# Sixteen adaLN modulation modules computed as row dot products on VectorE, from weights laid out by output column

## The chip, the cores and the metric

The kernel runs on one core of a Trainium2 chip. A core has a matrix engine (TensorE, PE in the profile), VectorE (DVE), ScalarE (ACT), GpSimd (POOL) and SyncE (SP), which here only issues transfers. The metric is the time of one execution on the device, in microseconds; the kernel before took 1797.8 us in the median of three runs.

## The reference, cut to what matters

Two layers of a diffusion backbone work on 256 latent tokens and 256 context tokens of 1024 features. Each layer is a half-step SwiGLU, a token mixing of four head groups, and another half-step SwiGLU. Each of these is modulated by nine vectors of 1024 (a shift, a scale and a gate for each of three sub-layers), one set from the condition `c` for the latent tokens and one from `c_ctx` for the context:

```python
for l in range(DEPTH):
    mx = jnp.split((jax.nn.silu(c) @ w_mod[l] + b_mod[l])[:, None, :], N_MOD, axis=-1)
    mz = jnp.split(jax.nn.silu(c_ctx) @ w_mod[l] + b_mod[l], N_MOD, axis=-1)
    x = x + 0.5 * mx[2] * swiglu(modulate(rms_norm(x), mx[0], mx[1]), ffn1_w1[l], ffn1_w3[l], ffn1_w2[l])
    z = z + 0.5 * mz[2] * swiglu(modulate(rms_norm(z), mz[0], mz[1]), ffn1_w1[l], ffn1_w3[l], ffn1_w2[l])
    ...   # token mixing with mx[3..5], second SwiGLU with mx[6..8]
```

`w_mod[l]` is a matrix of 1024 x 9216. So a modulation module (one of nine vectors of one layer) is a product of two rows of 1024 with a matrix of 1024 x 1024, 4 MB of f32 weights for very little arithmetic.

## The kernel before, in words

The activations lie transposed: features on the 128 partitions (eight tiles, `X[0]` to `X[7]`), 512 tokens along the free dimension. All large products are done in three passes: each weight tile and each activation is split into a high part (`whi`, `hh`, `gh`) and a low part (`wlo`, `hl`, `gl`), and `product` (L278 to L285) adds high x high, low x high and high x low in PSUM.

Weights come as one stream (`w_load` at L237 on SP's queue, three raw buffers); `w_conv` casts the high part on ACT (L248) and subtracts it on DVE for the low part (L251), some tiles ahead of the product that takes them.

In the SwiGLU (`ffn`) the 22 hidden tiles go in two groups of 12 and 10. For each hidden tile PE does the gate and the up projection (48 products), and `finish` applies silu on ACT (L408), multiplies on DVE (L410) and splits the result. Then for each of the eight output tiles PE does the down projection (36 products in the first group, 30 in the second) and DVE adds the result to `X` (L480).

Two of the eighteen modules, the shift and the scale of the very first norm, are computed at the start by PE (`mods_load`, `mods_first`). The other sixteen are the subject here. They are a generator, `mod_modules`, that runs in the background of three SwiGLUs: `step` takes two steps of it after each hidden tile and two after each down-projection tile. The first SwiGLU of layer 0 computes six modules, its second one four, the first SwiGLU of layer 1 six.

A module (`mod_module`) takes nine steps. In each of the first eight it loads 128 rows of the weights (a tile `wmod` of 128 x 1024, L163, three buffers) and adds them, scaled by the silu of the condition's feature on that partition, to an accumulator `macc` of 128 x 1024, for `c` and for `c_ctx`: the first time by a scaled copy on ACT (L166), then by multiply-adds on DVE (L169). What is left is a sum over partitions. The ninth step does it on PE: four products with ones (L174), a copy on ACT (L177), four transposes that bring the output column onto the partition (L180), and the bias on DVE (L184).

The order of instructions on each engine is made by a scheduler with a cost model of its own, from the program order, priorities and a few pins; `issue_after(behind())` puts the module's DVE instructions behind the latest low part of a weight.

Of the kernel before, what the change touches and what calls it, by code (L numbers as in the profile page):

```python
# [7 lines left out]
F32 = mybir.dt.float32  # L8
F32R = mybir.dt.float32r
U8 = mybir.dt.uint8  # L10
AF = mybir.ActivationFunctionType
ALU = mybir.AluOpType
# [3 lines left out]
P = 128  # L16
D = 1024
KD = 8
S = 256
T = 512  # L20
# [41 lines left out]
def bmid(ap, n):  # L62
    a = [list(x) for x in ap.ap]
    return bass.AP(tensor=ap.tensor, offset=ap.offset, ap=a[:-1] + [[0, n]] + a[-1:])
# [3 lines left out]
def tile_backbone(ctx: ExitStack, tc: tile.TileContext, a: dict, out: bass.AP):  # L68
    nc = tc.nc
# [7 lines left out]
    def bank(tag, name):  # L77
        return mm.tile([P, 512], F32, tag=tag, name=name, bufs=BANKS[tag])
# [4 lines left out]
    def small(n, name):  # L83
        return sp.tile([P, n], F32, tag=name, name=name, bufs=2 if name[0] in "de" else 8)

# [1 line left out]
    cin = cp.tile([P, KD, 32], F32, name="cin")  # L87
    nc.scalar.dma_start(out=cin, in_=a["cin"])
    cst = cp.tile([P, C_N], F32, name="cst")
# [1 line left out]
    bmod = cp.tile([P, 2, 72], F32, name="bmod")  # L91
# [21 lines left out]
    ident = cst[:, C_ID:C_ID + 128]  # L113
    ones = cp.tile([P, 128], F32, name="ones")
# [4 lines left out]
    sc = cin  # L119
# [1 line left out]

    mods = [cp.tile([P, 72, 2], F32, name=f"mod{l}") for l in range(2)]

# [1 line left out]
    def mods_load(q, pool, tiles):  # L125
        for k in range(KD):
            tag, n = ("wmod", 3) if q == 3 and k % 2 else (("gh", FA) if (q * KD + k) % 2 else ("gl", FA))
            if q < 3:
                raw = pool.tile([P, T], F32R, tag=tag, name="wfirst", bufs=FA).bitcast(F32)
            else:  # L130
                if k % 2 == 0:
                    raw2 = pool.tile([P, 2, 512], F32, tag="macc" if k == 0 else "wmod", name="wfirst", bufs=2 if k == 0 else 3)
                raw = raw2[:, k % 2, :]
            v = a["w_mod"][0, k * P:(k + 1) * P, 256 * q:256 * q + 256]
            nc.sync.dma_start(out=raw.rearrange("p (m c) -> p m c", m=2),
                              in_=bass.AP(tensor=v.tensor, offset=v.offset, ap=[list(v.ap[0]), [D, 2], list(v.ap[1])]))
            tiles.append(raw)
            yield
# [17 lines left out]
                                    in0=pt[:, :P].rearrange("p (m i s) -> p m i s", m=2, i=2)[:, :, :, 0:2],  # L156
                                    in1=bc(bmod[:, 0, 0:16].rearrange("p (m a i) -> p a m i", m=2, a=4)[:, q], 2), op=ALU.add)

    def mod_module(l, m, pool, behind):
        acc = pool.tile([P, 2, D], F32, tag="macc", name="macc", bufs=2)  # L160
        for k in range(KD):
            raw = pool.tile([P, 2, 512], F32, tag="wmod", name="wmod", bufs=3).rearrange("p a b -> p (a b)")
            nc.sync.dma_start(out=raw, in_=a["w_mod"][l, k * P:(k + 1) * P, m * D:(m + 1) * D])  # L163
            for s in range(2):
                if k == 0:
                    nc.scalar.activation(acc[:, s], raw, AF.Copy, scale=sc[:, k, s:s + 1])  # L166
                else:
                    with tc.issue_after(behind()):
                        nc.vector.scalar_tensor_tensor(out=acc[:, s], in0=raw, scalar=sc[:, k, s:s + 1], in1=acc[:, s],  # L169
                                                       op0=ALU.mult, op1=ALU.add)  # L170
            yield
        pm = bank("B", "pm")
        for j in range(4):
            nc.tensor.matmul(pm[32 * j:32 * j + 32, :], ones[:, 0:32], acc[:, j // 2, (j % 2) * 512:(j % 2) * 512 + 512],  # L174
                             start=True, stop=True)
        sb = pool.tile([P, T], F32, tag="g", name="modsb", bufs=2)
        nc.scalar.copy(sb, pm)  # L177
        pt = bank("B", "pmt")
        for i in range(4):
            nc.tensor.transpose(pt[:, i * P:(i + 1) * P], sb[:, i * P:(i + 1) * P], ident)  # L180
        dst = mods[l][:, 8 * m:8 * m + 8, :]
        src = pt.rearrange("p (i s j x) -> p s j i x", i=4, s=2, j=2)
        for s in range(2):
            nc.vector.tensor_tensor(out=dst.rearrange("p (j i) s -> p s j i", j=2)[:, s], in0=src[:, s, :, :, 0],  # L184
                                    in1=bmod[:, l, 8 * m:8 * m + 8].rearrange("p (j i) -> p j i", j=2), op=ALU.add)
        if m in (2, 8):
            nc.vector.tensor_scalar(out=dst, in0=dst, scalar1=0.5, scalar2=None, op0=ALU.mult)
        yield
# [1 line left out]
    def mcol(l, m, d, s):  # L190
        return mods[l][:, 8 * m + d, s:s + 1]

# [1 line left out]
    wlist = []  # L194

    def ffn_units(l, f):
# [10 lines left out]
    for l in range(2):  # L207
        ffn_units(l, 1)
        for u in ORDER:
# [6 lines left out]
            elif u in "RNQF":  # L216
                name, n = {"F": ("wfou", 2), "R": ("wgr", 2), "N": ("wna", 6), "Q": ("wgqa", 4)}[u]
# [8 lines left out]
    wlo = [None]  # L226
# [36 lines left out]
            w_load()  # L263
        return ready.pop(0)

# [1 line left out]
    def split_tiles(d):  # L267
        return (xp.tile([P, T], F32R, tag=f"hh{d}", name=f"hh{d}"),
                xp.tile([P, T], F32R, tag=f"hl{d}", name=f"hl{d}"))
# [23 lines left out]
        wh, wl = w[:2]  # L293
        product(((wh[:, k, :], xh), (wh[:, k, :], xl), (wl[:, k, :], xh)), ps, first, last)

# [1 line left out]
    def norm_square(st, pool, d, s0, s1, eng=nc.gpsimd):  # L297
        c = slice(s0 * S, s1 * S)
        if d == 0:
# [87 lines left out]
        st["apply"] = apply  # L387
        return st

# [1 line left out]
    def down_order(ns, split):  # L391
        tail = split if ns > 1 else 0
        return ([(mt, 0, ns) for mt in range(KD - tail)] +
# [86 lines left out]
            nc.vector.scalar_tensor_tensor(out=X[mt][:, c], in0=py[:, c], scalar=mcol(l, m, mt, s),  # L480
                                           in1=X[mt][:, c], op0=ALU.mult, op1=ALU.add)

# [1 line left out]
    def mixing(l, st, pool, npool):  # L484
        last = l == 1
        ntx = 2 if last else 4
# [56 lines left out]
            nc.vector.tensor_tensor(out=ov, in0=ps, in1=bc(rs[:, :n].rearrange("p (t h) -> p t h", t=2), 64), op=ALU.mult)  # L543
            return o

# [1 line left out]
        g = {}  # L547

        def gates():
# [168 lines left out]
                nc.vector.tensor_tensor(out=gr, in0=gr, in1=nn.rearrange("p (t n) -> p t n", t=2), op=ALU.mult)  # L718
                yield

# [1 line left out]
        def rev(ap):  # L722
            return ap.rearrange("p (b c) -> p b c", c=64)[:, :, ::-1]

# [122 lines left out]
            nc.scalar.copy(hh[:, c], src[:, c])  # L847
            eng.tensor_tensor(out=hl[:, c], in0=src[:, c], in1=hh[:, c].bitcast(F32), op=ALU.subtract)

# [1 line left out]
        nqT = [big(f"nqT{i}", tag=f"T{i}", bufs=1) for i in range(2)]  # L851
        nkS = [pool.tile([P, T], F32R, name=f"nkS{i}", bufs=1) for i in range(4)]
        nv = {}
# [44 lines left out]
                                           lambda e, t: head_bias(2 * hp + e, t), nqT[hp])  # L898
                    deliver(2 + hp, nqT[hp], p, nc.gpsimd)

# [1 line left out]
        def gq_norm(ps, nh, roff, rope):  # L902
            nn = rms_tok(ps, nh)
            w = nh * 64
# [45 lines left out]
                    yield from attend_pair(TAGS[1], p, [(gqT[kv], 0), (gqT[kv], 1)], [gkS[kv]] * 2, [vs] * 2, None, o)  # L950
                    deliver(6 + kv, o, p, nc.vector)

# [1 line left out]
        def fourier_in(U):  # L954
            U["c"] = [big("fou") for _ in range(2)]
            nc.sync.dma_start(out=U["c"][0], in_=a["fou"][:, F_L:F_L + 512])
# [38 lines left out]
            nc.scalar.copy(hh[:, :nx], pt[:, :nx])  # L995
            nc.vector.tensor_tensor(out=hl[:, :nx], in0=pt[:, :nx], in1=hh[:, :nx].bitcast(F32), op=ALU.subtract)

# [1 line left out]
        active = []  # L999

        def background():
# [44 lines left out]
        for i, u in enumerate(ORDER):  # L1046
# [5 lines left out]
            if u in streams:  # L1052
                gen, r = streams[u]
# [24 lines left out]
            evac(l, 5, mt, py, s0, s1)  # L1078
            after(mt, s0, s1)

# [1 line left out]
    def mod_modules(ms, pool):  # L1082
        for l, m in ms:
            yield from mod_module(l, m, pool, lambda: wlo[0])

    npool = ctx.enter_context(tc.tile_pool(name="norm", bufs=1))
    st = {"merge": False}
# [47 lines left out]
                ffn(l, 6, st2, n2, fp, npool, mod_modules([(0, 8)] + [(1, m) for m in range(3)], fp), fin)  # L1135


# [1 line left out]
def _constants():  # L1139
    import numpy as np  # L1140

# [38 lines left out]
def _arrays(inp):  # L1180
    import numpy as np

    g = {k: np.asarray(v) for k, v in inp.items()}
    f32 = np.float32
    r = {}
    xt = np.concatenate([g["x"][0], g["ctx"][0]], axis=0).T
    r["xin"] = xt.reshape(KD, P, T).transpose(1, 0, 2)
    cin = np.zeros((P, KD, 32), f32)
    cin[:, :, 0] = g["c"][0].reshape(KD, P).T
    cin[:, :, 1] = g["c_ctx"].reshape(KD, P).T  # L1190
    r["cin"] = cin
    r["w_mod"] = g["w_mod"]
    r["bmod"] = g["b_mod"].reshape(2, 72, P).transpose(2, 0, 1)

    def feat(w, c0, n, m):
        w = w[:, :, c0:c0 + n]
        return w.reshape(2, KD, P, n // m, m).transpose(0, 3, 2, 1, 4).reshape(2, n // m, P, KD * m)

    def tok(w, c0):
        w = w[:, :, c0:c0 + 256]  # L1200
        return w.reshape(2, 2, 4, P, 256).transpose(0, 1, 3, 2, 4).reshape(2, 2, P, 1024)

    for f in (1, 2):
        for w in (1, 3):
            r[f"f{f}w{w}"] = feat(g[f"ffn{f}_w{w}"], 0, NF * P, P)
        w2 = g[f"ffn{f}_w2"]
        r[f"f{f}w2"] = w2.reshape(2, NF, P, KD, P).transpose(0, 3, 2, 1, 4)
    w = g["w_in"]
    r["wgate"] = feat(w, 1792, 32, 32)[:, 0]
    r["wgqk"] = feat(w, 1024, 256, P)  # L1210
    r["wgv"], r["wgr"] = tok(w, 1280), tok(w, 1536)
    r["wna"] = np.concatenate([tok(w, c) for c in (256, 512, 768)], axis=1)
    r["wgqa"] = np.concatenate([tok(w, c) for c in (1824, 2080)], axis=1)
    r["wfou"] = tok(w, 0)
    r["wout"] = feat(g["w_out"], 0, D, P)
    vec = np.zeros((P, 2, 4), f32)
    row = np.zeros((2, P, R_N), f32)
    wg = np.zeros((P, 2, 2, 128), f32)
    for l in range(2):
        vec[:, l, V_NAQ] = np.tile(g["na_q_norm"][l], 2)  # L1220
        vec[:, l, V_NAK] = np.tile(g["na_k_norm"][l], 2)
        vec[:, l, V_BF] = g["gla_b_gate_f"][l]
        vec[:, l, V_BB] = g["gla_b_gate_b"][l]
        row[l, :, R_GQ:R_GQ + 256] = np.tile(g["gqa_q_norm"][l], 4)
        row[l, :, R_GK:R_GK + 128] = np.tile(g["gqa_k_norm"][l], 2)
        row[l, :, R_GN:R_GN + 256] = np.tile(g["gla_norm"][l], 4)
        for j in range(0, P, 32):
            wg[j:j + 16, l, 0] = g["gla_w_gate_f"][l]
            wg[j + 16:j + 32, l, 1] = g["gla_w_gate_b"][l]
    r["vec"], r["row"], r["wg"] = vec, row, wg  # L1230
    r["na_rpb"] = g["na_rpb"]
    r["cst"], r["fou"], r["lvl"] = _constants()
    return {k: np.ascontiguousarray(v) for k, v in r.items()}
# [19 lines left out]
```

## Time and profile before

| | |
|---|---|
| three runs | 1796.78, 1797.80, 1801.82 us (median 1797.8) |
| span of the profiled execution | 1797.1 us; the page gives no other time of it |
| PE busy | 1738.8 us (97%) |
| DVE busy | 1075.0 us (60%) |
| ACT busy | 703.8 us (39%) |
| mean granted TensorE clock | 0.989 of 2.4 GHz |
| chain that ended last | PE 90%, DMA 4%, DVE 3%, ACT 1% |
| transfers | 250.91 MB, 140 GB/s over the span |

The span runs from the first to the last instruction of one execution that the hardware profiler recorded. An engine's busy time counts the time in which one of its instructions was under way; PE's instructions overlap, so their mean durations don't add up to busy time, and the distance from one start to the next is the better measure of what one costs.

### The profile page before, as it was taken

What the parts mean: (1) busy time and instruction counts of PE and PEld (TensorE: products, weight loads), DVE (VectorE), ACT (ScalarE), POOL (GpSimd) and SP (SyncE); (2) the same over time, 40 slices, a digit from 0 to 9 for tenths busy, and PEclk for the clock granted to TensorE, in tenths of its full rate; (3) what the DMA queues carried; (4) which work ended last, traced back from release to release, by engine and by line L of the source; (5) the groups of instructions that cost most, each with busy time, mean ns of one, the idle gap of its engine ahead of it and who ended that gap; (6) DMA issues with size and microseconds to landing.
All of it is one profiled execution on the core that took longest, in us unless ns stands there. A gap on an engine that the chain in (4) does not pass through costs nothing.

```text
span 1797.1 us, 28107 instructions
## 1 busy us (share of the span) xinstructions
PE 1738.8 (97%) x11334; PEld 1484.1 (83%) x11334; DVE 1075.0 (60%) x1560; ACT 703.8 (39%) x1167; POOL 216.4 (12%) x259
## 2 busy tenths in 40 slices
PE   7999999998989999999999999999999897999999
PEld 5887888786978788887888888887888796889999
DVE  3566766635776667667333477676743476655554
ACT  4432233235645454322222343323223464554443
POOL 1000000012563230000000210000001344220000
PEclk9999999999999999999999999999999999999999
DMA  9455665334221136655332356566523333136664
GB/s 341 155 180 164 206 199 176 105 90 112 77 67 34 41 124 199 188 152 165 104 96 67 105 194 197 162 189 205 180 76 87 91 105 92 49 107 196 178 193 138
DMA packets 91843, 250.91 MB, mean 140 GB/s; under 512 B 17600, under 2 KB 28096, under 8 KB 91712
## 3 DMA queue, kind: packets, MB, share of 16 engines
q1 hardware_dynamic: 90128, 247.79, 45.6%
q8 instruction: 89, 1.46, 0.3%
q10 hardware_dynamic: 1584, 1.32, 0.2%
q14 instruction: 42, 0.34, 0.1%
HBM read 248.02 MB, written 1.05 MB: 139 GB/s over the span
## 4 chain that ended last, share of the span: by engine, by line
PE 90%; DMA 4%; DVE 3%; ACT 1%; issue 1%; POOL 1%; SPq 0%; POOLq 0%; DVEq 0%; ACTq 0%
PE p L285 47%; PE py L285 23%; PE pt L285 7%; PE pyo L285 3%; DMA bias<-in_na_rpb_dram 2%; PE pf L285 1%; PE po L790 1%; PE pm L174 1%; PE prT L781 1%; DVE wlo L251 1%; PE sc L758 1%; DMA wfirst<-in_w_mod_dram 1%; PE pg L554 1%; PE pa L674 1%; ACT whi L248 0%
## 5 line engine op out<-in xcount | busy, mean ns | idle before, releaser
L248 ACT CAST whi<-raw 128x1024 fp32r<-128x1024 f32 (+3 forms) x358 | 339.6, 950 | 826.3 <-PE p L285 297.3
L251 DVE TENSOR_TENSOR wlo<-raw,whi 128x1024 fp32r<-128x1024 f32 (+3 forms) x358 | 396.4, 1109 | 261.3 <-ACT whi L248 255.8
L285 PE MATMUL p<-hl,whi 128*128 128x512 f32 (+1 forms) x1504 | 528.5, 353 | 2.1 <-DVE hl L368 1.4
L285 PE MATMUL p<-hh,wlo 128*128 128x512 f32 (+1 forms) x1504 | 528.3, 352 | 0.0
L285 PE MATMUL p<-hh,whi 128*128 128x512 f32 (+1 forms) x1504 | 525.6, 353 | 1.3 <-ACT hh L363 1.1
L285 PEld LDWEIGHTS p<-hh,whi 128*128 128x128 f32 x1504 | 283.7, 190 | 47.0 <-issue 5.6
L285 PEld LDWEIGHTS p<-hl,whi 128*128 128x128 f32 x1504 | 285.9, 190 | 40.9 <-DVE hl L368 1.8
L285 PEld LDWEIGHTS p<-hh,wlo 128*128 128x128 f32 x1504 | 286.0, 190 | 37.5 <-DVE mod L155 0.2
L169 DVE SCALAR_TENSOR_TENSOR macc<-wmod,cin,macc 128x1024 f32<-128x1024 f32 x224 | 276.6, 1279 | 0.0
L285 PE MATMUL py<-gh,whi 128*128 128x512 f32 (+1 forms) x764 | 266.5, 350 | 0.0
L285 PE MATMUL py<-gl,whi 128*128 128x512 f32 (+1 forms) x764 | 265.5, 348 | 0.0
L285 PE MATMUL py<-gh,wlo 128*128 128x512 f32 (+1 forms) x764 | 265.2, 348 | 0.0
L312 POOL TENSOR_TENSOR ss<-ss,sq 128x512 f32<-128x512 f32 (+1 forms) x34 | 40.7, 1196 | 1095.6 <-ACT sq L309 1094.2
L410 DVE TENSOR_TENSOR g<-p,sl 128x512 f32<-128x512 f32 (+1 forms) x88 | 54.9, 624 | 187.3 <-PE p L285 174.6
L285 PEld LDWEIGHTS py<-gh,whi 128*128 128x128 f32 x764 | 143.4, 188 | 24.6 <-ACT whi L248 3.4
L285 PEld LDWEIGHTS py<-gl,whi 128*128 128x128 f32 x764 | 143.3, 188 | 20.4 <-issue 1.7
L285 PEld LDWEIGHTS py<-gh,wlo 128*128 128x128 f32 x764 | 143.5, 188 | 20.2 <-issue 0.8
L285 PE MATMUL pt<-whi,hl 128*128 128x256 f32 x448 | 132.3, 295 | 9.9 <-POOL hl L366 9.9
L285 PE MATMUL pt<-whi,hh 128*128 128x256 f32 x448 | 132.1, 295 | 0.5 <-DVE nm L762 0.5
L285 PE MATMUL pt<-wlo,hh 128*128 128x256 f32 x448 | 131.8, 294 | 0.0
L480 DVE SCALAR_TENSOR_TENSOR X<-py,mod,X 128x256 f32<-128x256 f32 x112 | 50.3, 480 | 105.0 <-PE py L285 104.8
L285 PEld LDWEIGHTS pt<-whi,hl 128*128 128x128 f32 x448 | 88.4, 197 | 19.5 <-POOL hl L366 13.6
(221 smaller groups left out, 1763.3 us busy)
## 6 DMA issues: line engine op xcount, KB each, us to landing
wmod<-in_w_mod_dram SPq DMA_DIRECT2D x128, 512.0 KB, 3.7
raw<-in_f1w_dram SPq DMA_DIRECT2D x88, 512.0 KB, 4.3
raw<-in_f2w_dram SPq DMA_DIRECT2D x88, 512.0 KB, 3.7
raw<-in_f1w_dram SPq DMA_DIRECT2D x32, 384.0 KB, 3.6
raw<-in_f2w_dram SPq DMA_DIRECT2D x32, 384.0 KB, 3.2
raw<-in_f1w_dram SPq DMA_DIRECT2D x32, 320.0 KB, 2.9
raw<-in_f2w_dram SPq DMA_DIRECT2D x32, 320.0 KB, 3.0
wfirst<-in_w_mod_dram SPq DMA_DIRECT2D x32, 256.0 KB, 6.5
```

What stands on the lines that cost most here:

```text
L169: nc.vector.scalar_tensor_tensor(out=acc[:, s], in0=raw, scalar=sc[:, k, s:s + 1], in1=acc[:, s], op0=ALU.mult, op1=ALU.add)
L174: nc.tensor.matmul(pm[32 * j:32 * j + 32, :], ones[:, 0:32], acc[:, j // 2, (j % 2) * 512:(j % 2) * 512 + 512], start=True, stop=True)
L248: nc.scalar.copy(hi[:, :k * n], raw[:, :k * n])
L251: wlo[0] = nc.vector.tensor_tensor(out=lo[:, :k * n], in0=raw[:, :k * n], in1=hi[:, :k * n].bitcast(F32), op=ALU.subtract).ins
L285: nc.tensor.matmul(ps, w, x, start=first and i == 0, stop=last and i == len(parts) - 1)
L312: (nc.vector if d == KD - 1 else eng).tensor_tensor(out=st["ss"][:, c], in0=st["ss"][:, c], in1=sq[:, c], op=ALU.add)
L410: nc.vector.tensor_tensor(out=g[:, :n], in0=p3[:, :n], in1=sl[:, :n], op=ALU.mult)
L480: nc.vector.scalar_tensor_tensor(out=X[mt][:, c], in0=py[:, c], scalar=mcol(l, m, mt, s), in1=X[mt][:, c], op0=ALU.mult, op1=ALU.add)
L554: nc.tensor.matmul(pg[j:j + 32, :], wf[:, k, :], h[k][0].bitcast(F32), start=k < 4, stop=4 < k)
L674: nc.tensor.matmul(pa[w * b:w * b + w, c * w:c * w + w], ke[hs, k0:k0 + w], qe[hs, q0:q0 + w], start=True, stop=True)
L758: nc.tensor.matmul(ps[:, :n], q[:, e, (t % 2) * P:(t % 2 + 1) * P], ks[e][:, T - n:T], start=i == 0, stop=i == 1)
L781: nc.tensor.transpose(pt[:, c * P:(c + 1) * P], pr[e][:, (2 * half + i) * P:(2 * half + i + 1) * P], ident)
```

## The change: what it does

The weights of the sixteen modules are laid out anew on the host, transposed: for a module and a tile of 128 output columns, the output column is on the partition and the 1024 input features lie along the row (`wmodt`). The condition is brought in as a row of 1024 for `c` and one for `c_ctx`, copied to all 128 partitions by one transfer (`crow`, 1 MB in SBUF), and its silu is taken on ACT, once in each of the three SwiGLUs. A module's step then loads one tile of 128 x 1024 and, for each of the two conditions, multiplies it by the row and sums along the row with one DVE instruction (`tensor_tensor_reduce`, which stands on DVE as two: the product and sum, and the read of the accumulator). Its result is a single column of 128 outputs, which is already where the modulation is used. The ninth step only adds the bias. The ones products, the copy, the transposes and the scaled copies on ACT are gone. The two modules at the start read their part of the weights from an array of their own (`wmodf`).

```diff
-    def mod_module(l, m, pool, behind):
-        acc = pool.tile([P, 2, D], F32, tag="macc", name="macc", bufs=2)
-        for k in range(KD):
-            raw = pool.tile([P, 2, 512], F32, tag="wmod", name="wmod", bufs=3).rearrange("p a b -> p (a b)")
-            nc.sync.dma_start(out=raw, in_=a["w_mod"][l, k * P:(k + 1) * P, m * D:(m + 1) * D])
+    def mod_module(l, m, pool, crow, behind):
+        acc = pool.tile([P, 2, KD], F32, tag="macc", name="macc", bufs=2)
+        for i in range(KD):
+            raw = pool.tile([P, D], F32, tag="wmod", name="wmod", bufs=3)
+            nc.sync.dma_start(out=raw, in_=a["wmodt"][l, m, i])
             for s in range(2):
-                if k == 0:
-                    nc.scalar.activation(acc[:, s], raw, AF.Copy, scale=sc[:, k, s:s + 1])
-                else:
-                    with tc.issue_after(behind()):
-                        nc.vector.scalar_tensor_tensor(out=acc[:, s], in0=raw, scalar=sc[:, k, s:s + 1], in1=acc[:, s],
-                                                       op0=ALU.mult, op1=ALU.add)
+                prod = pool.tile([P, D], F32, tag="mprod", name="mprod", bufs=2)
+                with tc.issue_after(behind()):
+                    nc.vector.tensor_tensor_reduce(out=prod, in0=raw, in1=crow[:, s], scale=1.0, scalar=0.0,
+                                                   op0=ALU.mult, op1=ALU.add, accum_out=acc[:, s, i:i + 1])
             yield
-        pm = bank("B", "pm")
-        for j in range(4):
-            nc.tensor.matmul(pm[32 * j:32 * j + 32, :], ones[:, 0:32], acc[:, j // 2, (j % 2) * 512:(j % 2) * 512 + 512],
-                             start=True, stop=True)
-        sb = pool.tile([P, T], F32, tag="g", name="modsb", bufs=2)
-        nc.scalar.copy(sb, pm)
-        pt = bank("B", "pmt")
-        for i in range(4):
-            nc.tensor.transpose(pt[:, i * P:(i + 1) * P], sb[:, i * P:(i + 1) * P], ident)
         dst = mods[l][:, 8 * m:8 * m + 8, :]
-        src = pt.rearrange("p (i s j x) -> p s j i x", i=4, s=2, j=2)
-        for s in range(2):
-            nc.vector.tensor_tensor(out=dst.rearrange("p (j i) s -> p s j i", j=2)[:, s], in0=src[:, s, :, :, 0],
-                                    in1=bmod[:, l, 8 * m:8 * m + 8].rearrange("p (j i) -> p j i", j=2), op=ALU.add)
+        nc.vector.tensor_tensor(out=dst.rearrange("p i s -> p s i"), in0=acc, in1=bmid(bmod[:, l, 8 * m:8 * m + 8], 2), op=ALU.add)
...
     def mod_modules(ms, pool):
+        crow = pool.tile([P, 2, D], F32, name="crow", bufs=1)
+        v = a["crow"]
+        nc.sync.dma_start(out=crow, in_=bass.AP(tensor=v.tensor, offset=v.offset, ap=[[0, P], [D, 2], [1, D]]))
+        nc.scalar.activation(crow, crow, AF.Silu)
         for l, m in ms:
-            yield from mod_module(l, m, pool, lambda: wlo[0])
+            yield from mod_module(l, m, pool, crow, lambda: wlo[0])
...
-    r["w_mod"] = g["w_mod"]
+    r["crow"] = np.stack([g["c"][0], g["c_ctx"]])
+    r["wmodf"] = g["w_mod"][0, :, :2 * D]
+    r["wmodt"] = g["w_mod"].reshape(2, D, 9, KD, P).transpose(0, 2, 3, 4, 1)
```

The scheduler orders the new program anew. Three places show what moved. On PE in the first SwiGLU, before, where the first module ends (`p` is a gate or up projection's PSUM tile, `hh` and `hl` the split activations):

```order
L285 MATMUL p_1177<-hl_632,whi 128x512
L285 MATMUL p_1177<-hh_631,wlo 128x512
L174 MATMUL pm<-macc,ones 32x512 x4
L285 MATMUL p_1266<-hh_289,whi 128x512
...
L285 MATMUL p_1266<-hl_632,whi 128x512
L180 MATMUL pmt<-cst,modsb 128x128 x4
L285 MATMUL p_1266<-hh_631,wlo 128x512
```

In the changed kernel the rows of L174 and L180 are gone, sixteen of each kind of group, and the products between them follow each other.

On DVE in the first down projection of layer 0, before (`X` is the residual update, `wlo` a weight's low part):

```order
L480 SCALAR_TENSOR_TENSOR X_83<-py,mod_97,X_83 128x256 x2
L251 TENSOR_TENSOR wlo<-raw,whi 128x768
L169 SCALAR_TENSOR_TENSOR macc<-wmod,cin,macc 128x1024 x4
L251 TENSOR_TENSOR wlo<-raw,whi 128x768
L480 SCALAR_TENSOR_TENSOR X_84<-py,mod_97,X_84 128x256 x2
```

And now, at the same place:

```order
L466 SCALAR_TENSOR_TENSOR X_83<-py,mod_97,X_83 128x256 x2
L237 TENSOR_TENSOR wlo<-raw,whi 128x768
L167 ISA mprod,macc<-wmod,crow 128x1024
L167 ISA macc 128x1
...
L237 TENSOR_TENSOR wlo<-raw,whi 128x768
L167 ISA mprod,macc<-wmod,crow 128x1024
L167 ISA macc 128x1
L466 SCALAR_TENSOR_TENSOR X_84<-py,mod_97,X_84 128x256 x2
```

Four module instructions stand in the step as before, each now with the read of its accumulator behind it, and one of them has moved behind the second low part.

On SP's queue at the start, before (`wfirst` are the pieces of the two modules at the start, `raw` the weight stream):

```order
L135 DMA wfirst<-in_w_mod_dram 128x2x256 x7
L237 DMA raw<-in_f1w_dram 128x1024
L135 DMA wfirst<-in_w_mod_dram 128x2x256 x9
...
L237 DMA raw<-in_f1w_dram 128x1024 x3
L163 DMA wmod<-in_w_mod_dram 128x1024 x3
L237 DMA raw<-in_f1w_dram 128x1024
```

And now:

```order
L135 DMA wfirst<-in_wmodf_dram 128x2x256
L223 DMA raw<-in_f1w_dram 128x1024
L135 DMA wfirst<-in_wmodf_dram 128x2x256 x15
...
L223 DMA raw<-in_f1w_dram 128x1024 x3
L1071 DMA crow<-in_crow_dram 128x2048
L163 DMA wmod<-in_wmodt_dram 128x1024 x3
L223 DMA raw<-in_f1w_dram 128x1024 x8
```

One weight load stands ahead of six more `wfirst` pieces than before, and the load of the condition's row stands in front of the first module weights. The same load stands in front of the first module loads of the two other SwiGLUs.

## Rows read from the trace of the kernel before

**Rows 1.** The page: span, and each engine's busy time, share and instructions.

```profile
span 1797.1 us, 28107 instructions
PE 1738.8 (97%) x11334; PEld 1484.1 (83%) x11334; DVE 1075.0 (60%) x1560; ACT 703.8 (39%) x1167; POOL 216.4 (12%) x259
```

**Rows 2.** Busy time by stretch: length, engines, granted clock, DMA share, GB/s.

```profile
225.00:270.00 45.00, 45.00 (x205) 36.23 (x204) 28.79 (x32) 14.07 (x17) 0.00 (x0) 1.00 0.66 198
750.00:800.00 50.00, 50.00 (x227) 40.43 (x226) 29.12 (x31) 17.17 (x23) 0.00 (x0) 1.00 0.54 162
1200.00:1250.00 50.00, 50.00 (x220) 39.25 (x219) 39.45 (x43) 13.44 (x15) 0.00 (x0) 1.00 0.68 210
```

**Rows 3.** The page's costliest groups: busy, mean ns, idle before and its releaser.

```profile
L248 ACT CAST whi<-raw 128x1024 fp32r<-128x1024 f32 (+3 forms) x358 | 339.6, 950 | 826.3 <-PE p L285 297.3
```

**Rows 4.** Groups by line and form: busy us, mean ns, idle before.

```profile
L251 DVE TENSOR_TENSOR wlo<-raw,whi 128x1024 fp32r<-128x1024 f32 x228 | 282.4, 1240 | 178.3 <-ACT whi L248 172.8
L169 DVE SCALAR_TENSOR_TENSOR macc<-wmod,cin,macc 128x1024 f32<-128x1024 f32 x224 | 276.6, 1279 | 0.0
...
L410 DVE TENSOR_TENSOR g<-p,sl 128x512 f32<-128x512 f32 x66 | 45.6, 691 | 170.5 <-PE p L285 158.3 <-issue 11.6 <-ACT sl L408 0.7
...
L166 ACT ACTIVATE macc<-wmod,cin 128x1024 f32<-128x1024 f32 x32 | 35.3, 1144 | 46.1 <-DMA wmod<-in_w_mod_dram 46.1
...
L174 PE MATMUL pm<-macc,ones 128*32 128x512 f32 x128 | 20.2, 605 | 0.0
...
L180 PE MATMUL pmt<-cst,modsb 128*128 128x128 f32 x64 | 9.6, 272 | 0.0
...
L762 DVE CUSTOM_DVE_ANT_0 pr<-sc,bias 128x512 f32<-128x512 f32 x8 | 5.5, 686 | 3.2 <-PE prT L781 2.9 <-PE sc L758 0.4
...
L583 DVE TENSOR_TENSOR_SCAN Bf<-ones,t 128x128 f32<-128x128 f32 x8 | 2.7, 402 | 0.0
...
L762 DVE DVE_READ_ACCUMULATOR2_ANT nm<- 128x1 f32 x16 | 1.3, 81 | 0.0
```

**Rows 5.** PE in order of time, first module's ones products: start, length, instruction.

```profile
127.65 0.39 PE L285 MATMUL p<-hh,whi 128*128 128x512 f32 x1
...
130.14 0.39 PE L285 MATMUL p<-hh,wlo 128*128 128x512 f32 x1
130.46 1.06 PE L174 MATMUL pm<-macc,ones 128*32 128x512 f32 x8
...
132.03 0.39 PE L285 MATMUL p<-hh,wlo 128*128 128x512 f32 x1
```

**Rows 6.** PE in order of time, the same module's transposes.

```profile
136.58 0.39 PE L285 MATMUL p<-hl,whi 128*128 128x512 f32 x1
136.81 0.60 PE L180 MATMUL pmt<-cst,modsb 128*128 128x128 f32 x4
...
137.48 0.39 PE L285 MATMUL p<-hh,whi 128*128 128x512 f32 x1
```

**Rows 7.** PE in order of time, ones products in two pieces.

```profile
172.27 0.40 PE L285 MATMUL py<-gh,whi 128*128 128x512 f32 x1
172.60 1.05 PE L174 MATMUL pm<-macc,ones 128*32 128x512 f32 x4
...
174.01 1.05 PE L174 MATMUL pm<-macc,ones 128*32 128x512 f32 x4
...
176.02 0.39 PE L285 MATMUL py<-gh,whi 128*128 128x512 f32 x1
```

**Rows 8.** DVE in order of time, a down-projection step with four multiply-adds.

```profile
1206.48 0.88 DVE L480 SCALAR_TENSOR_TENSOR X<-py,mod,X 128x256 f32<-128x256 f32 x2 [0.84 <-PE py L285]
...
1208.14 4.87 DVE L169 SCALAR_TENSOR_TENSOR macc<-wmod,cin,macc 128x1024 f32<-128x1024 f32 x4
...
1214.72 0.88 DVE L480 SCALAR_TENSOR_TENSOR X<-py,mod,X 128x256 f32<-128x256 f32 x2 [0.84 <-PE py L285]
```

**Rows 9.** The page's DMA issues: count, KB each, us to landing.

```profile
wmod<-in_w_mod_dram SPq DMA_DIRECT2D x128, 512.0 KB, 3.7
```

More of the change, by code (lines that the diff above doesn't have):

```diff
@@ L131, in mods_load @@
                 if k % 2 == 0:
-                    raw2 = pool.tile([P, 2, 512], F32, tag="macc" if k == 0 else "wmod", name="wfirst", bufs=2 if k == 0 else 3)
+                    raw2 = pool.tile([P, 2, 512], F32, tag="mprod" if k == 0 else "wmod", name="wfirst", bufs=2 if k == 0 else 3)
                 raw = raw2[:, k % 2, :]
-            v = a["w_mod"][0, k * P:(k + 1) * P, 256 * q:256 * q + 256]
+            v = a["wmodf"][k * P:(k + 1) * P, 256 * q:256 * q + 256]
             nc.sync.dma_start(out=raw.rearrange("p (m c) -> p m c", m=2),
```

## Prediction

> **What bounds the kernel now.** I read the busy line of the page first: TensorE (PE) is busy 1738.8 us of a span of 1797.1, VectorE (DVE) 1075.0, ScalarE (ACT) 703.8 [rows 1]. Two engines could set the time, so the next view is busy time by stretch. In three stretches in which modulation modules run, PE is busy for every microsecond of the stretch, at a granted clock of 1.00, while DVE has between a fifth and two fifths of it idle [rows 2]. A full PE could still be paced by the supply of split weights. The waits say no: the ACT casts that make the high halves stood idle 826.3 us, most of it until a PE product let a buffer go [rows 3]. The supply waits for PE, not PE for the supply. So in the module stages a PE instruction that goes is time that goes, for as long as DVE keeps up, and those are the two things to size.
>
> **What goes from PE.** A module ends with four ones products (L174, eight matmul records) and four transposes (L180). By groups of lines they hold PE 20.2 and 9.6 us in all [rows 4]. Busy time is modelled at its ends, so I take the cost from starts instead. From the first to the last of twelve products in a row the starts are 2.49 us apart, 0.2265 for each of the eleven intervals [rows 5]. Around the ones products of one module the starts stand 1.89 us apart where three intervals (0.68) would do: 1.21 us lost [rows 5]. Around the transposes it is 0.90 for two intervals: 0.45 [rows 6]. Three of the sixteen modules have their ones products in two pieces; there it is 3.75 for six intervals, 2.39 lost [rows 7]. Sum: 13 x 1.21 + 3 x 2.39 + 16 x 0.45 = 15.7 + 7.2 + 7.2 = 30.1 us, beside 29.8 by busy time. All of it lies in stretches with a full PE. The ACT copy and the small DVE additions between them go too; nothing waits for them there, and I count them at nothing.
>
> **What moves on ACT.** The 32 scalings that begin a module (1144 ns each, 36.6 us, with 46.1 us of waiting for the weights in front of them) leave the queue in which the casts stand [rows 4]. Three silus of 128x2048 come, about twice such a scaling, 2.3 us each. ACT idles over half of the span, so neither changes the time.
>
> **What DVE pays.** Gone are 224 multiply-adds, which start 1.20 us apart when four follow each other (4.87 us for four, the last one 1.28 long) [rows 4, 8]. In come 256 product-and-sum instructions, each followed by a read of the accumulator. The trace has this pair once, in the attention bias: 686 ns on 512 elements, with one operand in PSUM, and 81 ns for the read [rows 4]. From 512 to 1024 elements a plain two-operand operation grows from 691 to 1240 ns; so 686 + 549 = 1235 ns, and less the 0.08 us by which neighbours overlap (1.28 against 1.20) 1.15 us from start to start if the read hides, 1.23 if it doesn't. I take 1.20, the multiply-add's own, since the count of elements and operands is the same. The trace has no such instruction with both f32 operands in SBUF. The ends are 1.15 below (it can't pass its elements faster than the plain operation) and 3.2 above, from the one slow running form in the trace, the scan: 402 ns for 128 elements, eight times that [rows 4].
>
> At 1.20 DVE gets 256 x 1.20 - 224 x 1.20 = 38 us more work, against 722 us idle. The tight place is a down-projection step (two weight tiles, two residual updates, up to four module instructions). One such step of before lasted 8.24 us on DVE with 0.84 idle, and four multiply-adds fill 4.8 of it, which leaves 2.6 for the rest [rows 8]. PE needs 8.15 us per step (12 hidden tiles by three products, 36 x 0.2265). Four of the new ones fit while each takes less than (8.15 - 2.6) / 4 = 1.39 us. At 1.20 they do.
>
> **What the loads pay.** The weight traffic is the same. New are three loads of 1 MB, one row sent to all partitions, on SP's queue ahead of the first module loads. A wmod load of half that size lands in 3.7 us [rows 9], so such a load costs between nothing, where the casts have worked ahead, and 7.4 us, where they have not. Behind it on SP stand module loads, and weight loads that wait for a buffer anyway; on ACT a cast stands behind the silu. Before, a scaling waited for its weights at the same kind of place (46.1 us in all [rows 4]) and PE stayed full. At the start one weight load has also moved ahead of six pieces of the first modulation weights, at most one 3.7 us landing either way. I take +1 us for all of this.
>
> **The sum** is 1797.1 - 30.1 + 1 = 1768.0 for the span. The page gives no other time of that execution; the median of the runs is 0.7 above its span, so 1769 us.
>
> **The rule that speaks against the change.** The instruction with both operands in SBUF is the one thing not measured: with an operand in PSUM it runs at the rate of a plain operation, and the multiply-add with two f32 operands in SBUF does as well, without a sum [rows 4]. The Trainium skill (Vector Engine (DVE) Microarchitecture Reference, section "Points that are easy to get wrong") says that this family of instructions runs at half rate with two SBUF sources that are not bf16, as no read port is left for the accumulator. The multiply-add of this trace is such an instruction by its sources and isn't halved; no run here shows one that also sums. By the rule the sum would become that of the first rival.
>
> **Rivals.**
> *Half rate: slower.* Each product-and-sum takes 2 x 1.15 = 2.30 us. By the code two module steps follow each of 23 down-projection steps and 49 gate-and-up steps, and a module is nine steps with 16 instructions, so 3.56 stand in each on average. A down-projection step then needs 3.56 x 2.30 + 2.6 = 10.8 us on DVE against 8.15: 2.65 x 23 = 61 us. A gate-and-up step has 3.5 us of other DVE work (two tiles of 1240 and two of 691 ns, less the overlaps) and 48 x 0.2265 = 10.9 us of PE (two weights, eight tiles, three products): 11.7 against 10.9, 0.8 x 49 = 40 us. Time: 1769 + 101 = 1870. The gain is lost from 3.56 d + 2.6 - 8.15 = 30 / 23 on, d = 1.92 us. At the scan's 3.2 it would be near 2100. For it: no row has this form. Against it: the two rows that share one half of it each.
> *The starts give part of it back.* The three 1 MB loads stall weights behind them for half of their 7.4 us each: +11, 1780. For it: ACT's silu waits for the load with casts behind it. Against it: the casts' idle time [rows 3].
> *PE's free time isn't used,* since something else paces these stages: 1798. For it: DVE is at four fifths in the densest stretch. Against it: the casts wait for PE.
>
> **How the numbers follow.** Forecast 0.75 (its own range 1764 to 1775), half rate 0.09, starts 0.12, nothing gained 0.04. A change of under 0.3% (5.4 us) can't be told from none here. Faster are the forecast and nearly all of the starts case, 0.86; the same 0.05; slower 0.09. The range leaves out half rate, nothing gained and some 0.05 of tails: 1763 to 1786, which holds the starts case up to 17 us of stalls.
>
> **What would show it.** The profile after should have PE still full in the module stages, PE busy down by 30 us, the new DVE instruction near 1.25 us with a read near 80 ns, DVE busy up by some 40, and ACT casts still waiting for PE products. A DVE instruction above 1.4 us, or PE waiting for the low halves in down-projection steps, would make it wrong; so would PE idle for several microseconds at the three places where the row is loaded.

## The result, and the profile after

The changed kernel takes 1768.4 us in the median of four runs (1767.4 to 1770.4), against 1799.3 for the kernel before in four runs (1796.8 to 1801.8): a ratio of 0.9828, 95% interval 0.9814 to 0.9843. The forecast was 1769 with a range of 1763 to 1786. The profiled execution has a span of 1765.6 us.

The page's first lines (span, then busy time, share and instructions of each engine) answer to [rows 1]:

```profile
span 1765.6 us, 27971 instructions
PE 1708.3 (97%) x11142; PEld 1477.1 (84%) x11142; DVE 1100.2 (62%) x1832; ACT 667.3 (38%) x1122; POOL 216.5 (12%) x259
```

The span fell by 31.5 us and PE's busy time by 30.5, while DVE's grew by 25.2. PE is still at 97%: the gain is work taken off the engine that sets the time, not idle time removed.

Busy time in three stretches with module work (length, engines, granted clock, DMA share, GB/s), as in [rows 2]:

```profile
225.00:270.00 45.00, 45.00 (x199) 37.18 (x199) 33.81 (x54) 13.13 (x16) 0.00 (x0) 1.00 0.61 197
740.00:790.00 50.00, 50.00 (x222) 41.36 (x221) 35.13 (x53) 14.31 (x19) 0.00 (x0) 1.00 0.53 166
1165.00:1215.00 50.00, 50.00 (x220) 41.00 (x220) 41.03 (x68) 10.70 (x12) 0.00 (x0) 1.00 0.70 215
```

PE is full, DVE is 70 to 82% busy, ACT stands idle for most of it. The casts still wait for PE, which answers to [rows 3]:

```profile
L234 ACT CAST whi<-raw 128x1024 fp32r<-128x1024 f32 (+3 forms) x358 | 340.0, 951 | 893.5 <-PE p L271 289.2
```

The new groups by line and form (busy us, mean ns of one, idle before), beside those in [rows 4]:

```profile
L167 DVE CUSTOM_DVE_ANT_0 mprod<-wmod,crow 128x1024 f32<-128x1024 f32 x256 | 301.9, 1218 | 0.0
...
L167 DVE DVE_READ_ACCUMULATOR2_ANT macc<- 128x1 f32 x256 | 20.8, 81 | 0.0
...
L1072 ACT ACTIVATE crow<-crow 128x2048 f32<-128x2048 f32 x3 | 5.7, 1912 | 1.4 <-DMA crow<-in_crow_dram 1.4
```

A product-and-sum with both f32 operands in SBUF takes 1218 ns, a little less than the plain 1240 of a weight's low part. A down-projection step on DVE in order of time (start, length, instruction) shows what it costs from start to start, and answers to [rows 8]:

```profile
1167.53 0.87 DVE L466 SCALAR_TENSOR_TENSOR X<-py,mod,X 128x256 f32<-128x256 f32 x2 [1.97 <-PE py L271]
1168.32 0.95 DVE L237 TENSOR_TENSOR wlo<-raw,whi 128x768 fp32r<-128x768 f32 x1
1169.19 1.22 DVE L167 CUSTOM_DVE_ANT_0 mprod<-wmod,crow 128x1024 f32<-128x1024 f32 x1
1170.33 0.08 DVE L167 DVE_READ_ACCUMULATOR2_ANT macc<- 128x1 f32 x1
1170.33 1.22 DVE L167 CUSTOM_DVE_ANT_0 mprod<-wmod,crow 128x1024 f32<-128x1024 f32 x1
1171.48 0.08 DVE L167 DVE_READ_ACCUMULATOR2_ANT macc<- 128x1 f32 x1
...
1173.77 0.95 DVE L237 TENSOR_TENSOR wlo<-raw,whi 128x768 fp32r<-128x768 f32 x1
1175.77 0.88 DVE L466 SCALAR_TENSOR_TENSOR X<-py,mod,X 128x256 f32<-128x256 f32 x2 [1.05 <-PE py L271]
```

Four of them fill 1169.19 to 1173.77, 1.145 us each. The read of the accumulator and the next product start in the same hundredth, so the read costs nothing. The step has 1.05 us of idle left, where the one of before had 0.84.

The chain of waits (start, length, what) of before had a group of ones products and a group of transposes in it for each of the sixteen modules, six of them in the first SwiGLU. The first of these, beside [rows 5] and [rows 6]:

```profile
130.53 1.00 PE pm L174 x8
131.53 5.45 PE p L285 x23
136.98 0.44 PE pmt L180 x4
```

Through the first SwiGLU the chain of the changed kernel has no piece but products:

```profile
45.68 118.41 PE p L271 x560
164.09 65.94 PE py L271 x288
230.03 108.85 PE p L271 x480
338.88 50.41 PE py L271 x258
```

### The profile page after: what moved, and what is told of

It is laid out like the page before. It is cut to its first block, busy times and chain, and to the rows that moved or that the text cites. A ratio compares the mean times of both kernels' runs of the same rounds, so it can differ in the third digit from the quotient of the medians.

```text
span 1765.6 us, 27971 instructions
## 1 busy us (share of the span) xinstructions
PE 1708.3 (97%) x11142; PEld 1477.1 (84%) x11142; DVE 1100.2 (62%) x1832; ACT 667.3 (38%) x1122; POOL 216.5 (12%) x259
## 3 DMA queue, kind: packets, MB, share of 16 engines
HBM read 251.16 MB, written 1.05 MB: 143 GB/s over the span
## 4 chain that ended last, share of the span: by engine, by line
PE 89%; DMA 4%; DVE 3%; ACT 1%; issue 1%; POOL 1%; SPq 0%; POOLq 0%; DVEq 0%; ACTq 0%
PE p L271 48%; PE py L271 23%; PE pt L271 8%; PE pyo L271 3%; DMA bias<-in_na_rpb_dram 2%; PE pf L271 1%; PE po L776 1%; PE prT L767 1%; DVE wlo L237 1%; PE sc L744 1%; DMA wfirst<-in_wmodf_dram 1%; PE pa L660 1%; PE pg L540 0%; ACT whi L234 0%; DMA raw<-in_f1w_dram 0%
## 5 line engine op out<-in xcount | busy, mean ns | idle before, releaser
L167 DVE CUSTOM_DVE_ANT_0 mprod<-wmod,crow 128x1024 f32<-128x1024 f32 x256 | 301.9, 1218 | 0.0
```

The costliest lines, as they stand in the source:

```text
L167: nc.vector.tensor_tensor_reduce(out=prod, in0=raw, in1=crow[:, s], scale=1.0, scalar=0.0, op0=ALU.mult, op1=ALU.add, accum_out=acc[:, s, ...
```

## The experiments

All times are medians, and each ratio is to runs of the kernel before that were measured beside that experiment; their median was 1800.2 each time, where it was 1799.3 beside the changed kernel's 1768.4. A difference of one microsecond between two kernels is therefore not to be read as one. Each experiment starts from the kernel that its text names.

**1. Only PE's part of the change.** The kernel before, with the ones products, the copy and the transposes cut:

```diff
-        pm = bank("B", "pm")
...
-            nc.tensor.transpose(pt[:, i * P:(i + 1) * P], sb[:, i * P:(i + 1) * P], ident)
         dst = mods[l][:, 8 * m:8 * m + 8, :]
...
+        nc.vector.tensor_tensor(out=dst.rearrange("p i s -> p s i"), in0=acc[:, :, 0:KD], in1=bmid(bmod[:, l, 8 * m:8 * m + 8], 2), op=ALU.add)
```

> The kernel before with the sum over partitions left out: no ones products, no copy, no transposes on PE and ACT; the multiply-adds on DVE and the scalings on ACT stay as they are, and columns of the unsummed accumulator stand where the modulation should. Theory (the time is PE's slots): 30 us less than before, about 1769, the same as the changed kernel. Rival (the gain is ACT freed of the scalings that wait for weights, or DVE's new form): close to before, 1795 to 1800.

Measured: 1766.4 us, ratio 0.9818 (0.9802 to 0.9835); the expected 1769 lies within the interval. Its page and its groups show that DVE's multiply-adds and ACT's scalings, with 44.2 us of waiting for weights in front of them, are all still there:

```profile
span 1765.1 us, 27690 instructions
PE 1706.8 (97%) x11142; PEld 1474.8 (84%) x11142; DVE 1074.6 (61%) x1544; ACT 695.1 (39%) x1151; POOL 216.9 (12%) x259
```

```profile
L169 DVE SCALAR_TENSOR_TENSOR macc<-wmod,cin,macc 128x1024 f32<-128x1024 f32 x224 | 276.7, 1279 | 0.0
...
L166 ACT ACTIVATE macc<-wmod,cin 128x1024 f32<-128x1024 f32 x32 | 35.3, 1144 | 44.2 <-DMA wmod<-in_w_mod_dram 44.2
```

The whole gain is there without the new DVE instruction, the new layout or the scalings gone from ACT. That rival has fallen: what these moved was worth nothing that can be told from noise.

**2. PE's part put back.** The changed kernel with dead ones products and transposes:

```diff
+        pm = bank("B", "pm")
+        for j in range(4):
+            nc.tensor.matmul(pm[32 * j:32 * j + 32, :], ones[:, 0:32], crow[:, j // 2, (j % 2) * 512:(j % 2) * 512 + 512],
+                             start=True, stop=True)
+        pt = bank("B", "pmt")
+        for i in range(4):
+            nc.tensor.transpose(pt[:, i * P:(i + 1) * P], crow[:, 0, i * P:(i + 1) * P], ident)
         dst = mods[l][:, 8 * m:8 * m + 8, :]
```

> The changed kernel with the four ones products and four transposes of each module put back on PE, on the condition's row in place of the accumulator, their results unread. Theory: 16 x 1.21 + 16 x 0.45 = 26.6 us more than the changed kernel if each group stays in one piece, 30 with three in two pieces: 1795 to 1799. Rival (the gain came from ACT or DVE): within 3 us of the changed kernel's 1768.

Measured: 1797.0 us, ratio 0.9987 (0.9978 to 0.9997): 28.6 more than the changed kernel, though the copy on ACT was not put back. The chain of waits has the pieces back in it, though nothing reads their results:

```profile
257.62 1.00 PE pm L172 x8
258.61 0.37 PE pmt L176 x2
258.98 0.24 PE p L278
259.22 0.11 PE pmt L176
```

Work on a full engine costs its slots whether or not anyone waits for it.

**3. The disputed DVE price doubled.** Every product-and-sum and its read done twice:

```diff
-                with tc.issue_after(behind()):
-                    nc.vector.tensor_tensor_reduce(...)
+                for _ in range(2):
+                  with tc.issue_after(behind()):
+                      nc.vector.tensor_tensor_reduce(...)
```

> The changed kernel with each product-and-sum and its accumulator read done twice, so that a module column costs DVE 2.29 us (the half-rate rival's price). Theory A (each step must hold its own module work, as in the prediction): 61 + 38 us more, about 1867, with PE waiting for low halves in down-projection steps. Theory B (the module work may lag behind into steps with room): DVE has 338 us of work against 344 us of PE in the first SwiGLU, so under 20 us more, 1770 to 1788.

Measured: 1798.9 us, ratio 0.9989 (0.9978 to 1.0), 30 more than the changed kernel: neither theory's number, and 70 less than the first rival's price. Busy time by stretch (PE, PEld, DVE, ACT, POOL, clock, DMA share, GB/s) shows the first SwiGLU and the start of the mixing after it, here:

```profile
45.00:389.00 344.00, 344.00 (x1591) 287.06 (x1589) 317.93 (x502) 97.79 (x129) 11.09 (x8) 1.00 0.53 165
389.00:430.00 41.00, 25.80 (x138) 22.34 (x136) 41.00 (x77) 14.90 (x32) 13.77 (x13) 0.67 0.23 73
```

and in the changed kernel:

```profile
45.00:389.00 344.00, 344.00 (x1591) 287.20 (x1591) 228.80 (x353) 99.07 (x132) 9.38 (x9) 1.00 0.53 169
389.00:430.00 41.00, 35.85 (x214) 27.87 (x213) 23.19 (x41) 21.78 (x39) 12.79 (x17) 0.96 0.44 116
```

In the SwiGLU PE is as full as in the changed kernel and does the same 1591 matmuls, down-projection steps and all: PE never waits there. The price falls in the 41 us behind it, where DVE is busy to the last and PE, short of normed activations, does 138 matmuls in place of 214. The first product `g` on DVE in the next SwiGLU starts at 690.58 us, in the changed kernel at 671.90: 18.7 us of the price arise up to there. From the last `g` of layer 1's first SwiGLU to the first `X` update of the mixing behind it the doubled kernel takes 233.9 us, the changed one 224.7: another 9.2. The module work alone (DVE busy, clock, DMA share, GB/s) shows why; these are stretches of the doubled kernel, the last of them around the end of layer 1's first SwiGLU:

```profile
345.00:389.00 44.00, 30.30 (x43) 1.00 0.52 157
389.00:430.00 41.00, 24.42 (x40) 0.67 0.23 73
...
1385.00:1430.00 45.00, 14.78 (x24) 0.85 0.33 84
```

Of the six modules computed in the first SwiGLU only the first, its gate, is needed there, so the scheduler was free to let the others lag, and on DVE what lagged past the end stands among the instructions of the next norm. In the changed kernel no module work is left in any of the three stretches. The waits of the 41 us (who waited for whom, us, times, longest) name the norm:

```profile
ACT hh L350 <- DVE htmp L348: 13.0, 3, 6.8
...
PEld pb L311 <- DVE ss L299: 11.3, 2, 7.7
PE pb L311 <- DVE ss L299: 10.8, 2, 7.5
```

In the changed kernel the second and third of these waits don't stand in that stretch, and the first is half as long:

```profile
ACT hh L349 <- DVE htmp L347: 6.7, 4, 2.6
```

So theory B has the mechanism, and its size was too small: it left out what the overhang does to the norm.

**4. The same with half the extra work** (`range(1 + s)` in place of `range(2)`):

> The changed kernel with the product-and-sum of the second condition done twice: 1.72 us of DVE for a module column on average. Theory A (each down-projection step must hold its module work): 3.56 x 1.72 + 2.6 - 8.15 = 0.57 us in 23 steps, 13 us more than the changed kernel, 1781. Theory B (the work lags, and costs only what it lags past the end of its SwiGLU): in the changed kernel the first SwiGLU's module work ends at 341.5 of 389 us and with all of it doubled at 419; half of that lag ends at about 380, before the end: 1767 to 1771, and no module work on DVE after the last down projection.

Measured: 1771.4 us (1769.2 to 1771.9), ratio 0.9835 (0.9809 to 0.9861), 3 above the changed kernel's median and 0.4 above the range that theory B gave; it excludes theory A's 1781. The module work, in the first two stretches as above, is done in time, at 346.3 us:

```profile
345.00:389.00 44.00, 1.23 (x2) 1.00 0.31 94
389.00:430.00 41.00, 0.00 (x0) 0.96 0.41 115
```

It was expected to end near 380, half of the way between its end in the changed kernel (342.7) and that with all of it doubled (425.1). So the lag doesn't grow in proportion to the work, and theory B's step from one to the other was wrong. I did not find a place for the 3 us. By the ratios it is 1.2 us, well within the interval, and the kernel of experiment 6 without the row's load, which does no more on DVE than the changed one, has nearly the same span in its profile (1769.2 beside 1769.3).

**5. The doubled work spread.** As experiment 3, with one module moved to the SwiGLU before:

```diff
-                ffn(l, 6, st2, n2, fp, npool, mod_modules([(0, 8)] + [(1, m) for m in range(3)], fp), fin)
+                ffn(l, 6, st2, n2, fp, npool, mod_modules([(0, 8)] + [(1, m) for m in range(4)], fp), fin)
...
-                ffn(l, 0, st, T, fp, npool, mod_modules([(1, m) for m in range(3, 9)], fp), after)
+                ffn(l, 0, st, T, fp, npool, mod_modules([(1, m) for m in range(4, 9)], fp), after)
```

> Each product-and-sum done twice, and one module of layer 1 moved from its first SwiGLU to the second SwiGLU of layer 0 (five and five in place of four and six). Theory B (the loss is module work that lags past the end of a SwiGLU into the token mixing): the loss at the mixing of layer 1, 9 us, goes, the 19 us at the mixing of layer 0 stay: 1787 to 1791. Theory A (the loss follows the amount of DVE work): unchanged, 1797 to 1800.

Measured: 1787.9 us (1787.2 to 1792.5), ratio 0.9934 (0.9910 to 0.9959): 11 less than experiment 3 with the same amount of DVE work. Module work of this kernel, behind the first SwiGLU of layer 0 and around the end of layer 1's:

```profile
389.00:430.00 41.00, 24.55 (x40) 0.75 0.23 72
...
1385.00:1430.00 45.00, 0.00 (x0) 0.96 0.35 84
```

The overhang of layer 1 (14.78 us in experiment 3) is gone, that of layer 0 is not. The profile is of the slowest of the four runs; in it the next SwiGLU's first `g` starts 23.0 us later than in the changed kernel, and the stretch of layer 1 that was 9.2 us longer in experiment 3 is 0.5 longer. So the loss follows the overhang, not the sum.

**6. The row's loads taken away and doubled.** Once a fill in place of the load, once 1 MB more behind it:

```diff
-        nc.sync.dma_start(out=crow, in_=bass.AP(tensor=v.tensor, offset=v.offset, ap=[[0, P], [D, 2], [1, D]]))
+        nc.gpsimd.memset(crow, 0.5)
```

> The changed kernel without the three 1 MB loads of the condition's row: the row is filled with 0.5 by GpSimd instead, so the modulation is not that of the condition. Theory (the loads are hidden): within 1.5 us of the changed kernel, 1767 to 1769. Rival (the starts give part of the gain back): 11 us less, 1757, up to 22 less.

Measured: 1769.0 us (1766.6 to 1774.0), ratio 0.9838 (0.9815 to 0.9860).

```diff
+        for s in range(2):
+            more = pool.tile([P, D], F32, tag="mprod", name="more", bufs=2)
+            nc.sync.dma_start(out=more, in_=bass.AP(tensor=v.tensor, offset=v.offset + s * D, ap=[[0, P], [1, D]]))
```

> The changed kernel with 1 MB more loaded behind each of the three loads of the condition's row (the row again, into buffers that the products use later). Theory (hidden): 1767 to 1771. Rival (the loads at the starts cost time): 11 us more, 1779, up to 22.

Measured: 1768.5 us (1767.6 to 1769.2), ratio 0.9821 (0.9800 to 0.9842). In the changed kernel the row's three loads land 8.3, 4.2 and 7.4 us after their issue, the first above the 7.4 that the prediction had as the upper end; in this one the pieces behind them land after 8.1 in the median (name, count, KB, median us to landing; first the changed kernel, then this one):

```profile
crow<-in_crow_dram SPq DMA_DIRECT2D x3, 1024.0 KB, 7.4
```

```profile
crow<-in_crow_dram SPq DMA_DIRECT2D x3, 1024.0 KB, 5.9
more<-in_crow_dram SPq DMA_DIRECT2D x6, 512.0 KB, 8.1
```

Neither moved the time by more than the intervals leave open, and both exclude the 11 us: the loads are hidden, at twice their size too, and the starts case has fallen.

## Why the prediction was right, step by step

- **PE's slots, 30.1 us.** Right in mechanism and size. PE busy fell by 30.5; cutting the slots alone gave 1766.4, putting them back 28.6 of 30. The sum from starts (30.1) and the one from busy time (29.8) can't be told apart by these runs.
- **The last step of the sum.** That the time came out within 1 us of 1769 is in part luck. The span was to be 1768.0 and is 1765.6, 2.4 less. The prediction then added 0.7, the distance from the profiled span of before to the median of its runs; every run on record takes 1.7 to 1.9 us longer than its own span, and the median here lies 2.8 above the profiled one. The two misses nearly cancel.
- **DVE's product-and-sum, 1.20 us.** It came out at the low end of its bounds, 1.145 beside 1.15, since the read hides. DVE got 25.2 us more, not 38, so this term was put too high. The size didn't matter here: a step has room for 5.5 us of module work by the prediction, and four products take 4.6. The limit of 1.39 us a product that was worked out from this room is wrong: in experiment 4 a module column costs 1.72 us on average and the time is the same within the noise.
- **The rule of the skill.** The trace's row is 1218 ns for 1024 elements with both f32 operands in SBUF, as against 1240 for a plain two-operand instruction: not halved. The Trainium skill (Vector Engine (DVE) Microarchitecture Reference, section "Points that are easy to get wrong") says that the shape `S2S2D2_STT` has half the throughput with two SBUF sources that are not bf16. The page doesn't name the product-and-sum, and the trace shows no half rate for it.
- **ACT.** Its busy time fell by 36.5 us, and experiment 1 gets the gain with all its scalings in place. The silu took 1.9 us, not 2.3.
- **The loads, +1 us.** The chain's long run of products begins at 45.68 us; in the kernel before a piece of the same kind began at 44.79. These 0.9 us can't be put down to the change: in experiment 1, which has the loads of before in their order, the run begins at 45.44. Removing or doubling the row's load changed nothing that can be measured. So no run shows the +1 us, and it is too small to be told from none.
- **The half-rate rival, 1870 us.** Its condition didn't come about, but experiment 3 made its price and gave 1799. The step that failed is "a down-projection step then needs 10.8 us on DVE against 8.15": it took module work to be bound to its step. It is bound only to the end of its SwiGLU. That made no difference to the forecast, since at 1.145 us neither bound is reached. The point from which the gain is lost is not 1.92 us a product but near 2.29, where experiment 3 stands level with the kernel before.
- **What stays open.** The span fell 1.0 us further than PE's busy time. Even where no module work hangs over, spans differ by some microseconds with no cause that was looked for: from the last `g` of layer 1's first SwiGLU to the first `X` update of the mixing the changed kernel takes 224.7 us, that of experiment 6 without the row's load 226.7.

## What to carry to other kernels

On an engine that is full for a whole stage, count the starts that an instruction pushes back, and expect that time back when it goes, even if nobody waits for its result. Before pricing extra work on an engine with room, ask when its results are due: here, background work that the scheduler could delay cost nothing that could be told from noise until it hung over the end of the stage, and then it cost what it added to the next stage's first waits. Where an engine's added work can be doubled cheaply, one such run gives the margin better than an estimate.

## What the runs showed of the hardware

- The read of an accumulator (81 ns) behind a product-and-sum starts together with the next product, so the pair takes 1.145 us from start to start, where the multiply-add of the kernel before took 1.20.
- One row of 8 KB sent to 128 partitions (1 MB) landed in 7.4 us in the median of three, twice the 3.7 of a load of half the size from 128 different rows: reading the same bytes 128 times was no slower per byte. The three range from 4.2 to 8.3, with other loads under way, so this is a rough comparison.
- In experiment 3 the granted clock was 1.00 in the SwiGLU and 0.67 in the mean of the 41 us behind it, between the two levels of 2.4 and 1.2 GHz; PE had been full before and was busy for 25.8 of these 41 us. In the changed kernel the same stretch has PE busy 35.85 of 41 and a clock of 0.96. Part of an overhang's price is thus a slower PE: the 128x256 down-projection products of this stretch took 333 to 361 ns in the mean of each kind, against 277 to 288 in the changed kernel. How much of the 18.7 us that is was not taken apart.
